# Start-up of a two-layer mixer trunk: the parameter rows copied ahead of the first weight splits, x's squares behind the memory's copies, x spilled in four pieces

## The chip, the cores and the metric

The kernel runs on one core of one Trainium2 chip, as one program. The metric is its time on the device in microseconds (us), from one launch with all inputs in the chip's memory. Beside the times there is one profiled execution, of which every instruction is recorded.

The engines of a core that the text speaks of: TensorE (PE, matmuls and transposes), VectorE (DVE), ScalarE (ACT), GpSimd (POOL) and SyncE (SP, which here only issues transfers). PSUM is the memory that matmuls write to. Each engine takes its own instructions in the order of its queue.

## The reference, cut to what matters

Two layers; x is 512 tokens of 1024 numbers, `mem` is 256 tokens of 1024.

```python
def reference(x, mem, positions, norm_mix, w_in, ..., mem_norm, mem_w_kv, ...):
    mem_n = rmsnorm(mem, mem_norm)
    for l in range(2):
        x = hybrid_layer(x, mem_n, ...)

def hybrid_layer(x, mem_n, ...):
    h = rmsnorm(x, norm_mix)
    (...) = split_cols(h @ w_in)                       # 1024 x 9416
    ...                                                # four branches y_a, y_b, y_c, and:
    mk, mv = jnp.split(mem_n @ mem_w_kv, 2, axis=-1)   # 1024 x 1024
    mk = rmsnorm(mk.reshape(b, 256, 4, 128), mem_k_norm)
    ...                                                # y_m: attention of x's queries to mk, mv
    x = x + merged @ w_out
    hf = rmsnorm(x, norm_ffn)
    gate, up = jnp.split(hf @ ffn_w_up, 2, axis=-1)
    return x + (jax.nn.silu(gate) * up) @ ffn_w_down
```

The change concerns what comes before the first `h @ w_in`: the normed memory, its keys and values for both layers, and the first `h`.

## The kernel before, in words

**Products.** Every fp32 matrix product is done in three matmuls (`mm3`, lines 284 to 286): both operands are split in a high part (rounded to the matmul's format) and a low part (the rest), and hi·hi, hi·lo and lo·hi are summed in PSUM. So each weight and each activation passes through a split: ScalarE writes the high part by a copy, VectorE writes the low part by a subtraction.

**Weights.** `Chunk` loads 1024 x 256 weights (1 MB) by SyncE's queue into `w_raw` (two buffers). It is split in two halves of 4 rows of tiles each, `w_hi` on ScalarE and `w_lo` on VectorE, each with three buffers, so a split waits until TensorE has done with the half three before it. `A()` (line 119) is the helper through which every ScalarE operation goes, so that line stands for them all; the tiles tell them apart.

**Start-up.** The parameter rows (norm gains and the like) come by small loads into `rows`, one transpose (line 184) brings them into PSUM, and a ScalarE copy writes them to `prm`, one column to each 128 channels. Then, as the program is written:

- `mem_in_T()`: the memory is transposed (line 402) in eight steps. Each step writes `mt_hi` (ScalarE, scaled by a column of `prm`) and `mt_lo` (VectorE). The first step's scaling thus needs `prm`.
- `mem_kv(0)` with `first_h()`, step about, then `rope_tables()` and `mem_kv(1)`, all of which share the engines. Each `mem_kv` runs over four weight chunks, eight in all ("chunk 1" to "chunk 8"). A chunk is multiplied with both 128-token halves of the memory (`tokens`), 24 matmuls of 128x256 for each, 48 a chunk, 384 in all. For keys, ScalarE copies the result out of PSUM into `ku`, it is normed, transposed back, and split into `kv`; for values it is split into `kv` straight from PSUM. The results take turns in three PSUM tiles (`mm`). The finished `kv` goes out to memory on ScalarE's queue.
- `first_h()`: x is loaded into `xin` (two loads). ScalarE squares it in four instructions that also sum (written to `mem_sq`, sums to `xs`); from the sums come `rstd`, and four small matmuls spread it (line 429). Then for each of eight chunks x is transposed (line 436), copied to `xc`, and split into `h_hi` and `h_lo` (`h_chunk`, line 297). At the end `xc`, 2 MB, is stored to `x_spill` by one transfer on ScalarE's queue (line 441), to be read back for the residual.

Then the first layer's mixer begins: chunks of `w_in`, multiplied with `h`, with 128x512 matmuls.

**What sets the order.** The program's text names tiles and operations; a list scheduler with a model of the engines' times puts each engine's instructions in a row before the kernel is compiled. `tc.high_priority(offset=AHEAD)` lets the weight splits and the `ku` copies be chosen ahead of what is written before them. The row that comes out is fixed: on the chip an engine waits at an instruction whose input is not there, whatever stands behind it.

Of the kernel before, what the change touches and what calls it, by code (L numbers as in the profile page):

```python
# [16 lines left out]
AF = mybir.ActivationFunctionType  # L17
# [7 lines left out]
D = 1024  # L25
KD = D // P
DEPTH = 2
MEM = 256
# [41 lines left out]
def hybrid_trunk(ctx: ExitStack, tc: tile.TileContext, x, mem, positions, norm_mix, w_in, conv_w,  # L70
                 dsa_q_norm, dsa_k_norm, hgrn_lower_bounds, hgrn_out_norm, mem_norm, mem_w_kv,
                 mem_q_norm, mem_k_norm, w_lift, w_out, norm_ffn, ffn_w_up, ffn_w_down, out):
    nc = tc.nc
# [33 lines left out]
    order = mybir.DependencyInfo(mybir.DependencyClass.NoSync, mybir.DependencyReason.DATA)  # L107
# [4 lines left out]
    def A(dst, src, func, **kw):  # L112
        name = tables.get(func)
        if name is not None and name != table["set"]:
            load = act.preload_act_table_set(name)
            for u in table["users"]:
                tc.add_manual_dep(load.ins, u.name, order, reason="table set")
            table.update(set=name, load=load.ins, users=[])
        i = act.activation(dst, src, func, **kw)  # L119
        if name is not None:  # L120
            tc.add_manual_dep(i.ins, table["load"].name, order, reason="table set")
            table["users"].append(i.ins)
        return i
# [7 lines left out]
    def tr_ps():  # L131
        return bank["tr"]()

    def f(ap):
        return ap.bitcast(F32)
# [28 lines left out]
    ps = tr_ps()  # L164
# [3 lines left out]
    n_rows = 78  # L168
# [13 lines left out]
    prm = consts.tile([P, n_rows], F32, name="prm")  # L182
    ps = tr_ps()
    pe.transpose(ps[:, :n_rows], rows[:n_rows, :], ident[:n_rows, :n_rows])
    A(prm, ps[:, :n_rows], AF.Copy)

    def g_mix(l, c):
        return prm[:, l * KD + c:l * KD + c + 1]
# [4 lines left out]
    def g_mem(c):  # L193
        return prm[:, 32 + c:33 + c]
# [28 lines left out]
    def rstd_into(dst, ms, scratch, n):  # L223
        rstd(dst, ms, scratch(n), scratch(n))

    def small(n, name="small", bufs=12):
        return consts.tile([P, 8], F32, name=name, bufs=bufs)[:, :n]
# [8 lines left out]
    class Chunk:  # L236
        def __init__(self, src, kt, n):
            self.kt, self.step = kt, min(kt, 1024 // n)
            raw = wpool.tile([P, 2048], F32, name="w_raw", bufs=RAW_BUFS)[:, :kt * n].rearrange("p (k n) -> p k n", n=n)
            nc.sync.dma_start(raw, src.rearrange("(k p) n -> p k n", p=P))  # L240
            self.parts = []
            for k in range(0, kt, self.step):
                e = min(kt, k + self.step)
                m = (e - k) * n
                hi, lo = (wpool.tile([P, 1024], F32R, name=nm, bufs=W_BUFS)[:, :m].rearrange("p (k n) -> p k n", n=n)
                          for nm in ("w_hi", "w_lo"))
                with tc.high_priority(offset=AHEAD):
                    A(hi, raw[:, k:e], AF.Copy)
                    dve.tensor_sub(lo, raw[:, k:e], f(hi))  # L249
                self.parts.append((range(k, e), hi, lo))  # L250

        def at(self, k):
            hi, lo = self.parts[k // self.step][1:]
            return hi[:, k % self.step, :], lo[:, k % self.step, :]
# [33 lines left out]
    x_dram = nc.dram_tensor("x_spill", [P, KD, S], F32, kind="Internal").ap()  # L288
# [6 lines left out]
    def h_chunk(h, ssq, c, gain, xs):  # L295
        A(h[0][:, c, :], xs, AF.Copy, scale=gain)
        dve.scalar_tensor_tensor(h[1][:, c, :], xs, gain, f(h[0][:, c, :]), op0=OP.mult, op1=OP.subtract)
        if ssq is not None:
            square(ssq, c, xs)
# [94 lines left out]
    mem_sq = sp.tile([P, D], F32, name="mem_sq")  # L394
    mt = (sp.tile([P, KD, MEM], F32R, name="mt_hi"), sp.tile([P, KD, MEM], F32R, name="mt_lo"))
    mem_r2, mem_r4 = small(4, name="mem_r2", bufs=1), small(4, name="mem_r4", bufs=1)

    def mem_in_T():
        for c in range(KD):
            ps = tr_ps()  # L400
            for t in range(2):
                pe.transpose(ps[:, t * P:(t + 1) * P], mem_in[:, t, c * P:(c + 1) * P], ident)
            A(mt[0][:, c, :], ps[:, :MEM], AF.Copy, scale=g_mem(c))
            dve.scalar_tensor_tensor(mt[1][:, c, :], ps[:, :MEM], g_mem(c), f(mt[0][:, c, :]),
                                     op0=OP.mult, op1=OP.subtract)
        for t in range(2):
            A(mem_sq, mem_in[:, t, :], AF.Square, scale=D ** -0.5, accum_out=mem_ss[:, t:t + 1])
        rstd_into(mem_r, mem_ss, small, 2)
        dve.tensor_copy(mem_r4.rearrange("p (a b) -> p a b", b=2), mem_r[:, :, None].to_broadcast([P, 2, 2]))
        dve.tensor_mul(mem_r2, mem_r4, mem_r4)  # L410
# [3 lines left out]
    def first_h():  # L414
        xin = sp.tile([P, NT, D], F32, name="xin")
        for hf in range(2):
            nc.sync.dma_start(xin[:, 2 * hf:2 * hf + 2, :],
                              x[0, hf * 2 * P:(hf + 1) * 2 * P, :].rearrange("(t p) d -> p t d", p=P))
        xs = small(NT, "xs", 1)
        r_t = small(NT, "rstd_t", 2)  # L420
        r_b = state.tile([P, S], F32, name="rstd", bufs=1)
        for t in range(NT):
            A(mem_sq, xin[:, t, :], AF.Square, scale=D ** -0.5, accum_out=xs[:, t:t + 1])
        rstd_into(r_t, xs, small, NT)
        ps = tr_ps()
        for t in range(NT):
            diag = sp.tile([P, P], F32, name="diag", bufs=2)
            dve.tensor_scalar(diag, ident, r_t[:, t:t + 1], float(P), op0=OP.mult, op1=OP.mult)
            pe.matmul(ps[:, t * P:(t + 1) * P], ones_h, diag, start=True, stop=True)
        A(r_b, ps, AF.Copy)  # L430
        norms.extend((r_t, r_b))
        xc = sp.tile([P, KD, S], F32, name="xc")
        for c in range(KD):
            ps = tr_ps()
            for t in range(NT):
                pe.transpose(ps[:, t * P:(t + 1) * P], xin[:, t, c * P:(c + 1) * P], ident)
            A(xc[:, c, :], ps, AF.Copy)
            h_chunk(h, None, c, g_mix(0, c), xc[:, c, :])
            if c % 2:
                yield  # L440
        nc.scalar.dma_start(x_dram, xc)

    def mem_kv(l):
        kv = sp.tile([P, 4, 2, 2, MEM], F32R, name="kv", bufs=1)
# [29 lines left out]
        for q in range(2):  # L474
# [8 lines left out]
            nc.scalar.dma_start(kv_dram[l][:, 2 * q:2 * q + 2, 1], f(kv[:, 2 * q:2 * q + 2, 1]))  # L483
            yield
    mem_in_T()
    steps(mem_kv(0), first_h())
    rope_tables()
    steps(mem_kv(1))
# [861 lines left out]
```

## Time and profile before

| | |
|---|---|
| time, median of 3 runs | 2039.63 us (2039.58 to 2039.97) |
| the profiled execution's own time | 2039.99 us |
| its span in the profile | 2038.3 us |
| mean clock granted to TensorE | 0.994 of full speed |
| TensorE busy | 2011.1 us (99% of the span), 10440 matmuls |
| VectorE busy | 1418.7 us (70%) |
| ScalarE busy | 1112.4 us (55%) |
| moved by the DMA queues | 226.93 MB, 111 GB/s on average |

The profile of one execution gives the busy time of each engine, the groups of instructions by line and tile, the waits of an engine with what ended them, and the chain of waits: the work that ended last, followed back from the end, at each step to what released it. The timeline lists an engine's instructions with start and duration. Where neighbours of one kind follow closely they stand in one row with a count, and the records of neighbours overlap a little. A table by windows gives for stretches of the span how long each engine was busy, the clock granted to TensorE and what the transfers moved.

### The profile page before, as it was taken

Reading aid. Unit: us, or ns where it says so; the run is one execution under the profiler, and the core shown is the slowest. Engines: PE = TensorE matmul, PEld = TensorE weight load, DVE = VectorE, ACT = ScalarE, POOL = GpSimd, SP = SyncE. Lnnn points to the kernel's source line nnn. Section 1 sums busy time; section 2 is a strip of 40 time slices with the busy share of each in tenths; the row PEclk is TensorE's granted clock in tenths of the full one; section 3 lists DMA queues with packets and bytes.
Section 4 is the critical chain, followed back from the end, with each engine's and each line's share of the span. In section 5 each row is a group of like instructions: output and inputs, shape, how many; then the busy total and the mean of one; then the engine's idle time right before and its main releaser. Section 6 shows DMA issues by size and latency. Waiting matters only on the chain.

```text
span 2038.3 us, 27510 instructions
## 1 busy us (share of the span) xinstructions
PE 2011.1 (99%) x10440; PEld 1695.1 (83%) x10440; DVE 1418.7 (70%) x2721; ACT 1112.4 (55%) x1978; POOL 68.9 (3%) x84
## 2 busy tenths in 40 slices
PE   7899999999999999999999999999999999999999
PEld 7898988888888878888889898878888887888887
DVE  5668899636766778547656889964677577863772
ACT  6554565866666555324445455577667655542541
POOL 1000000000000011001000000000000001000100
PEclk8899999999999999999999999999999999999999
DMA  6632122212224475525352222221222337563442
GB/s 222 231 94 89 57 94 93 94 63 66 90 73 144 113 198 133 146 93 135 98 176 72 91 78 94 94 93 42 83 73 83 129 112 186 151 156 103 104 114 93
DMA packets 177847, 226.93 MB, mean 111 GB/s; under 512 B 5922, under 2 KB 131956, under 8 KB 177588
## 3 DMA queue, kind: packets, MB, share of 16 engines
q1 hardware_dynamic: 160800, 193.55, 29.0%
q0 software_dynamic: 13312, 23.21, 7.0%
q10 hardware_dynamic: 3604, 8.43, 1.1%
q8 instruction: 82, 1.34, 0.3%
q14 instruction: 49, 0.40, 0.1%
HBM read 214.67 MB, written 10.49 MB: 110 GB/s over the span
## 4 chain that ended last, share of the span: by engine, by line
PE 94%; DMA 3%; DVE 1%; ACT 1%; issue 0%; POOL 0%; SPq 0%; ACTq 0%; DVEq 0%; POOLq 0%
PE mm L284 19%; PE mm L285 18%; PE mm L286 18%; PE B L285 4%; PE B L286 4%; PE B L284 4%; PE A L286 4%; PE A L284 4%; PE A L285 4%; PE C L285 2%; PE C L284 2%; PE C L286 2%; DMA w_raw<-in_ffn_w_up_dram 1%; PE tr L734 1%; PE tr L728 1%; PE at L705 1%
## 5 line engine op out<-in xcount | busy, mean ns | idle before, releaser
L119 ACT ACTIVATE w_hi<-w_raw 128x1024 fp32r<-128x1024 f32 (+1 forms) x362 | 373.5, 1033 | 448.3 <-PE mm L285 137.4
L249 DVE TENSOR_TENSOR w_lo<-w_raw,w_hi 128x1024 fp32r<-128x1024 f32 x258 | 311.8, 1209 | 224.4 <-ACT w_hi L119 221.1
L284 PE MATMUL mm<-h_hi,w_hi 128*128 128x512 f32 x960 | 378.7, 395 | 0.0
L285 PE MATMUL mm<-h_lo,w_hi 128*128 128x512 f32 x960 | 377.3, 393 | 0.0
L286 PE MATMUL mm<-h_hi,w_lo 128*128 128x512 f32 x960 | 375.3, 393 | 0.0
L284 PEld LDWEIGHTS mm<-h_hi,w_hi 128*128 128x128 f32 x960 | 180.5, 188 | 37.4 <-issue 2.0
L286 PEld LDWEIGHTS mm<-h_hi,w_lo 128*128 128x128 f32 x960 | 180.4, 188 | 37.3 <-issue 0.7
L285 PEld LDWEIGHTS mm<-h_lo,w_hi 128*128 128x128 f32 x960 | 180.5, 188 | 36.7 <-issue 1.7
L1132 DVE TENSOR_TENSOR w_lo<-w_raw,w_hi 128x1024 fp32r<-128x1024 f32 (+1 forms) x104 | 117.8, 1138 | 61.4 <-ACT w_hi L119 61.2
L286 PE MATMUL mm<-w_hi,h_lo 128*128 128x256 f32 (+1 forms) x448 | 127.9, 286 | 0.0
L284 PE MATMUL mm<-w_hi,h_hi 128*128 128x256 f32 (+1 forms) x448 | 127.1, 285 | 0.0
L285 PE MATMUL mm<-w_lo,h_hi 128*128 128x256 f32 (+1 forms) x448 | 126.9, 284 | 0.0
L284 PE MATMUL mm<-y_hi,w_hi 128*128 128x512 f32 x256 | 102.3, 401 | 0.0
L286 PE MATMUL mm<-y_hi,w_lo 128*128 128x512 f32 x256 | 101.5, 397 | 0.0
L285 PE MATMUL mm<-y_lo,w_hi 128*128 128x512 f32 x256 | 101.3, 396 | 0.0
L119 ACT ACTIVATE w_hi<-f_raw 128x1024 fp32r<-128x1024 f32 (+1 forms) x64 | 62.7, 980 | 60.8 <-PE B L286 38.5
L286 PEld LDWEIGHTS mm<-w_hi,h_lo 128*128 128x128 f32 x448 | 85.6, 191 | 1.4 <-issue 0.8
L284 PEld LDWEIGHTS mm<-w_hi,h_hi 128*128 128x128 f32 x448 | 85.2, 191 | 1.2 <-issue 0.8
L285 PEld LDWEIGHTS mm<-w_lo,h_hi 128*128 128x128 f32 x448 | 85.4, 191 | 0.7
L1132 DVE TENSOR_TENSOR w_lo<-f_raw,w_hi 128x1024 fp32r<-128x1024 f32 (+1 forms) x64 | 71.6, 1120 | 11.8 <-ACT w_hi L119 11.4
L119 ACT ACTIVATE prob<-prob,small 128x128 f32<-128x128 f32 (+3 forms) x128 | 69.2, 554 | 15.4 <-DVE small L717 14.8
L285 PE MATMUL B<-w_lo,s_hi 128*128 128x512 f32 (+1 forms) x192 | 71.7, 375 | 1.1 <-DVE w_lo L1132 1.1
(425 smaller groups left out, 4563.6 us busy)
## 6 DMA issues: line engine op xcount, KB each, us to landing
w_raw<-in_w_in_dram SPq DMA_DIRECT2D x72, 1024.0 KB, 5.1
w_raw<-in_ffn_w_up_dram SPq DMA_DIRECT2D x60, 512.0 KB, 4.5
w_raw<-in_ffn_w_down_dram SPq DMA_DIRECT2D x18, 1024.0 KB, 5.6
w_raw<-in_w_lift_dram SPq DMA_DIRECT2D x32, 512.0 KB, 3.4
w_raw<-in_ffn_w_up_dram POOLq DMA_DIRECT2D x24, 512.0 KB, 6.0
f_raw<-in_ffn_w_up_dram SPq DMA_DIRECT2D x20, 512.0 KB, 4.5
w_raw<-in_mem_w_kv_dram SPq DMA_DIRECT2D x8, 1024.0 KB, 7.8
w_raw<-in_w_out_dram SPq DMA_DIRECT2D x8, 1024.0 KB, 5.1
```

The source lines that it names most:

```text
L119: i = act.activation(dst, src, func, **kw)
L249: dve.tensor_sub(lo, raw[:, k:e], f(hi))
L284: pe.matmul(ps, ah, bh, start=first, stop=False, skip_group_check=go_on)
L285: pe.matmul(ps, ah, bl, start=False, stop=False, skip_group_check=go_on)
L286: pe.matmul(ps, al, bh, start=False, stop=last, skip_group_check=go_on)
L705: pe.matmul(ps, q[:, hh, s], k[1][:, :n], start=False, stop=True)
L728: pe.transpose(pp[:, (2 * e + i) * P:(2 * e + i + 1) * P], probs[2 * i + e][:, b * P:(b + 1) * P], ident)
L734: pe.matmul(pv[e * HD:(e + 1) * HD, :], vt[:, b, :], pt[:, b, e * 2 * P:(e + 1) * 2 * P], start=b == 0, stop=b == t)
L1132: dve.tensor_sub(lo, self.raw[:, 2 * i:2 * i + 2, :], f(hi))
```

## The change

Two things are changed. First, three orders between ScalarE's instructions are laid down for the scheduler, as dependencies that fix an order and add no wait between engines: the `w_hi` splits of chunk 1 come behind the copy to `prm`; every later `w_hi` split, and the four squares of `xin`, come behind the last `mt_hi` copy. Second, `xc` is stored in four transfers of 512 KB, each issued after the two chunks that it holds, where it was one of 2 MB at the end.

```diff
-    A(prm, ps[:, :n_rows], AF.Copy)
+    first = {"prm": A(prm, ps[:, :n_rows], AF.Copy)}
+
+    def behind(i, *names):
+        for n in names:
+            tc.add_manual_dep(i.ins, first[n].ins.name, order, reason="first work")
...
                 with tc.high_priority(offset=AHEAD):
-                    A(hi, raw[:, k:e], AF.Copy)
+                    behind(A(hi, raw[:, k:e], AF.Copy), "mt" if "w" in first else "prm")
                     dve.tensor_sub(lo, raw[:, k:e], f(hi))
                 self.parts.append((range(k, e), hi, lo))
+            first["w"] = True
...
-            A(mt[0][:, c, :], ps[:, :MEM], AF.Copy, scale=g_mem(c))
+            first["mt"] = A(mt[0][:, c, :], ps[:, :MEM], AF.Copy, scale=g_mem(c))
...
         for t in range(NT):
-            A(mem_sq, xin[:, t, :], AF.Square, scale=D ** -0.5, accum_out=xs[:, t:t + 1])
+            behind(A(mem_sq, xin[:, t, :], AF.Square, scale=D ** -0.5, accum_out=xs[:, t:t + 1]), "mt")
...
             h_chunk(h, None, c, g_mix(0, c), xc[:, c, :])
             if c % 2:
+                nc.scalar.dma_start(x_dram[:, c - 1:c + 1, :], xc[:, c - 1:c + 1, :])
                 yield
-        nc.scalar.dma_start(x_dram, xc)
```

The diff moves lines by up to five: L240 becomes L244, L249 L253, L441 L445. The rows that the scheduler makes differ on each engine in the start-up and the first part of the first mixer only.

ScalarE at the start, before, from the first small norm operation of the memory (`small`) on. `w_hi_215` and `w_hi_219` are chunk 1's halves; `mem_sq, xs <- xin` are the squares of x.

```order
L119 ACTIVATE small_203<-mem_ss_154,eps_82 128x2
L119 ACTIVATE w_hi_215<-w_raw_213 128x1024
L119 ACTIVATE w_hi_219<-w_raw_213 128x1024
L119 ACTIVATE small_203<-small_203,half_84 128x2
L119 ACTIVATE small_204<-small_203 128x2
L119 ACTIVATE mem_sq_156,xs_314<-xin_311 128x1024 x3
L119 ACTIVATE prm_132<-tr_133 128x78
L119 ACTIVATE mem_sq_156,xs_314<-xin_311 128x1024
L119 ACTIVATE mt_hi_157<-tr_161,prm_132 128x256
```

The same place now, as far as the first square. Eight `mt_hi` copies stand between chunk 1's splits and chunk 2's; their last three end the first piece shown here.

```order
L119 ACTIVATE small_203<-mem_ss_154,eps_82 128x2
L119 ACTIVATE small_203<-small_203,half_84 128x2
L119 ACTIVATE small_204<-small_203 128x2
L119 ACTIVATE prm_132<-tr_133 128x78
L119 ACTIVATE w_hi_215<-w_raw_213 128x1024
L119 ACTIVATE w_hi_219<-w_raw_213 128x1024
L119 ACTIVATE mt_hi_157<-tr_161,prm_132 128x256
```

```order
L119 ACTIVATE mt_hi_157<-tr_186,prm_132 128x256
L119 ACTIVATE mt_hi_157<-tr_191,prm_132 128x256
L119 ACTIVATE mt_hi_157<-tr_196,prm_132 128x256
L119 ACTIVATE w_hi_362<-w_raw_360 128x1024
L119 ACTIVATE w_hi_366<-w_raw_360 128x1024
L119 ACTIVATE mem_sq_156,xs_314<-xin_311 128x1024
```

The copy to `prm` has moved ahead of chunk 1's splits and of all squares; the squares have moved behind the eight `mt_hi` copies and both halves of chunk 2 (`w_hi_362`, `w_hi_366`). On VectorE, chunk 1's two `w_lo` now stand ahead of the first `mt_lo`:

```order
L253 TENSOR_TENSOR w_lo_216<-w_raw_213,w_hi_215 128x1024
L253 TENSOR_TENSOR w_lo_220<-w_raw_213,w_hi_219 128x1024
L409 SCALAR_TENSOR_TENSOR mt_lo_158<-tr_161,prm_132,mt_hi_157 128x256
```

Before, they stood ahead of it too, with nine rows of other small work between the second and the `mt_lo`; now none.

ScalarE near the end of the start-up, before. `w_hi_978` is chunk 8's second half, `w_hi_1103` the first half of the first `w_in` chunk, `ku_877` the copy that frees the PSUM tile which chunk 8's first 24 matmuls (`mm_982`) need.

```order
L119 ACTIVATE h_hi_152<-xc_342,prm_132 128x512 x2
L441 DMA x_spill<-xc_342 128x4096
L119 ACTIVATE w_hi_978<-w_raw_972 128x1024
L119 ACTIVATE kv_710<-mm_917,mem_r_155 128x2x128
L119 ACTIVATE kv_710<-mm_944,mem_r_155 128x2x128
L119 ACTIVATE w_hi_1103<-w_raw_1101 128x1024
L119 ACTIVATE ku_877<-mm_852 128x256
```

The same place now, where the numbers are three or so higher (`w_hi_981`, `w_hi_1106`, `ku_880`), from the third piece of the spill to the fourth:

```order
L445 DMA x_spill<-xc_342 128x1024
L119 ACTIVATE w_hi_981<-w_raw_975 128x1024
L119 ACTIVATE xc_342<-tr_622 128x512
L119 ACTIVATE xc_342<-tr_630 128x512
L119 ACTIVATE kv_713<-mm_920,mem_r_155 128x2x128
L119 ACTIVATE h_hi_152<-xc_342,prm_132 128x512
L119 ACTIVATE w_hi_1106<-w_raw_1104 128x1024
L119 ACTIVATE kv_713<-mm_947,mem_r_155 128x2x128
L119 ACTIVATE kv_713<-tr_801,prm_132 128x256
L119 ACTIVATE h_hi_152<-xc_342,prm_132 128x512
L119 ACTIVATE ku_880<-mm_855 128x256
L445 DMA x_spill<-xc_342 128x1024
```

The last two `xc` copies and the last `h_hi` copies, all ahead of chunk 8's second half before, now stand behind it; the split of `w_in` still stands ahead of the `ku` copy, with two `kv` copies and one `h_hi` between. The tile that this `ku` copy frees is now needed by chunk 8's second 24 matmuls (`mm_1012`); the first 24 (`mm_985`) wait for VectorE alone. The first piece of the spill stands ahead of chunk 7's second half, the second and third behind chunk 8's first half, the fourth behind the `ku` copy.

## The prediction

> **What bounds the kernel.** I read the page first, then TensorE's waits, then the chain of waits in its first 90 us, because the diff touches only the start-up. "Kept busy" below means that the rows show no gap.
>
> ```profile
> span 2038.3 us, 27510 instructions
> PE 2011.1 (99%) x10440; PEld 1695.1 (83%) x10440; DVE 1418.7 (70%) x2721; ACT 1112.4 (55%) x1978; POOL 68.9 (3%) x84
> PE 94%; DMA 3%; DVE 1%; ACT 1%; issue 0%; POOL 0%; SPq 0%; ACTq 0%; DVEq 0%; POOLq 0%
> PE tr L402 <- ACT prm L119: 6.5, 1, 6.5
> PE mm L284 <- ACT ku L119: 5.9, 1, 5.9
> PE tr L468 <- DVE ku L464: 1.2, 1, 1.2
> 84.00:90.00 6.00, 6.00 (x33) 4.92 (x32) 5.54 (x23) 2.56 (x5) 0.00 (x0) 1.00 0.56 172
> ```
>
> TensorE is busy 99% of the span and carries 94% of the chain. So an edit pays only where TensorE stands still. Its waits (engine and line, who released it, us in total, times, longest) show two long ones in the start-up: 6.5 us for the ScalarE copy that writes `prm`, and 5.9 us for a ScalarE copy that writes `ku`. From 84 us on it is full at clock 1.00 (columns of the last row: PE, weight loads, VectorE, ScalarE, GpSimd, granted clock, DMA share, GB/s). Behind that point the order of the program is soon the old one, so I count no change there: what the first mixer matmul gains, the end gains.
>
> **Step 1, the start: `prm` ahead of the squares.** ScalarE's and TensorE's timelines (start, duration, instruction, idle before):
>
> ```profile
> 10.41 0.36 PE L184 MATMUL tr<-ident,rows 78*128 78x78 f32 x1 [3.45 <-DMA rows<-n_hgrn_lower_bounds_dram]
> 11.22 2.00 ACT L119 ACTIVATE w_hi<-w_raw 128x1024 fp32r<-128x1024 f32 x2 [1.93 <-DMA w_raw<-in_mem_w_kv_dram]
> 16.79 1.06 ACT L119 ACTIVATE mem_sq<-xin 128x1024 f32<-128x1024 f32 x1 [0.36 <-DMA xin<-in_x_dram]
> 17.84 0.22 ACT L119 ACTIVATE prm<-tr 128x78 f32<-128x78 f32 x1
> 19.02 0.82 ACT L119 ACTIVATE mt_hi<-tr,prm 128x256 fp32r<-128x256 f32 x2
> 19.53 0.58 PE L284 MATMUL mm<-w_hi,mt_hi 128*128 128x256 f32 x1 [0.73 <-ACT mt_hi L119]
> ```
>
> The transposed parameter rows are in PSUM at about 10.8 (10.41 + 0.36). The copy to `prm` starts at 17.84, because ScalarE takes its queue in order and three squares of `xin` stand ahead, the third of which waits for its load until 16.79. In the new order stand `prm`, the two `w_hi` of chunk 1, then the `mt_hi` copies. The `w_hi` splits still wait for their load at 11.22 and take 2.00; the first `mt_hi` thus starts near 13.2 instead of 19.02, 5.8 us earlier.
>
> Two pieces come off. On VectorE the first `mt_lo` stands behind chunk 1's two `w_lo`, which run straight ahead of it when `mt_hi` comes this early; I take 0.4 for the matmul that reads it. Chunk 2's first split stood behind three `mt_hi` copies and now stands behind all eight; a split takes about 1.0 us, half of which the 48 matmuls of chunk 1 should hide: 0.5. Together 0.9, bounds 0 and 1.5 (none hidden, and 0.5 for `mt_lo`). The slow clock of the first matmuls is the same on both sides. **Step 1: 5.8 − 0.9 = 4.9 us.**
>
> **Step 2, the squares.** They move into a stretch in which TensorE is full, so they need room on ScalarE (groups with count, busy us, mean ns and idle before; then a window's row, a row of the chain, and two matmuls from the end of this stretch):
>
> ```profile
> L119 ACT ACTIVATE w_hi<-w_raw 128x1024 fp32r<-128x1024 f32 x18 | 19.0, 1059 | 9.7 <-DMA w_raw<-in_w_in_dram 6.1 <-DMA w_raw<-in_mem_w_kv_dram 2.3 <-PE mm L286 1.2
> L119 ACT ACTIVATE mem_sq<-xin 128x1024 f32<-128x1024 f32 x4 | 4.2, 1056 | 0.8 <-DMA xin<-in_x_dram 0.8
> L119 ACT ACTIVATION_READ_ACCUMULATOR mem_sq<-xin 128x1 f32 x4 | 0.7, 187 | 0.0
> 20.00:30.00 10.00, 10.00 (x74) 10.00 (x74) 6.84 (x24) 5.00 (x12) 0.00 (x0) 0.83 0.13 41
> 62.35 1.23 DVE w_lo L249
> 68.02 0.28 PE L285 MATMUL mm<-w_lo,mt_hi 128*128 128x256 f32 x1
> 68.14 0.28 PE L286 MATMUL mm<-w_hi,mt_lo 128*128 128x256 f32 x1
> ```
>
> 4.2 + 0.7 = 4.9 us in records that overlap a little. Where they land ScalarE has been busy 5.00 of 10 us (20 to 30), so the idle half of that stretch hides them. The risk is position: they stand between splits. A chunk's second half is needed 24 matmuls after its first, 24 × 0.12 = 2.9 us (the pitch of the two matmul rows); its `w_hi` and `w_lo` take 1.06 + 1.23 = 2.3. One square of 1.06 + 0.19 ahead of it oversteps that by 0.6, unless the split started early. With four squares the cost lies between 0 and 4.9; I take 0.3, near the lower end, because the stretch has 5 us free. The chain norms → `rstd` → `xc` starts later too, but is not on the path: first matmuls on `h` come only after 384 matmuls.
>
> **Step 3, the second stall: the spill and the first w_in chunk.**
>
> ```profile
> 57.65 0.45 PE tr L436 x4
> 61.10 0.27 ACT ku L119
> 61.37 0.96 ACT w_hi L119
> 63.61 11.37 DMA w_raw<-in_w_in_dram
> 64.13 0.34 ACTq L441 DMA_DIRECT2D x_spill<-xc  x1
> x_spill<-xc ACTq DMA_DIRECT2D x1, 2048.0 KB, 10.7
> w_raw<-in_mem_w_kv_dram SPq DMA_DIRECT2D x8, 1024.0 KB, 7.8
> w_raw<-in_mem_w_kv_dram SPq DMA_DIRECT2D x1, 1024.0 KB, 5.1
> 75.06 1.06 ACT L119 ACTIVATE w_hi<-w_raw 128x1024 fp32r<-128x1024 f32 x1 [6.13 <-DMA w_raw<-in_w_in_dram]
> 76.03 0.37 ACT L119 ACTIVATE ku<-mm 128x256 f32<-128x256 f32 x1
> 76.45 0.58 PE L284 MATMUL mm<-w_hi,mt_hi 128*128 128x256 f32 x1 [5.93 <-ACT ku L119]
> 71.00:72.00 1.00, 0.00 (x0) 0.00 (x0) 0.00 (x0) 0.00 (x0) 0.00 (x0) 0.58 1.14 485
> 81.00:82.00 1.00, 1.00 (x9) 1.00 (x9) 0.63 (x5) 0.21 (x1) 0.00 (x0) 0.80 0.00 0
> 84.47 0.40 PE L284 MATMUL mm<-h_hi,w_hi 128*128 128x512 f32 x1
> ```
>
> The first rows are the chain's (start, us, what), then come an issue and three groups of issues (the last of 28 to 34 us alone), timelines and windows. They read: behind a `w_lo` (the chain's row above) a `w_raw` buffer comes free at 63.6, the w_in load goes out, and 0.5 us later the whole 2 MB spill goes out beside it. The load takes 11.37 us (the eight mem_w_kv loads: median 7.8). Its split stands ahead of a `ku` copy on ScalarE; that copy would free the PSUM tile which chunk 8's first matmul needs. So TensorE ends at 68.3 and resumes at 76.45: 8.2 us, less 0.45 for four `ku` transposes in the gap (the duration of the L436 row): 7.7. Then the clock: it falls to 0.50 at about 71.2 (0.58 over 71 to 72) and is back at about 81.4 (0.80 over 81 to 82). The last 48 matmuls took 84.47 − 76.45 = 8.02 us; at 0.12 each they take 5.76: 2.26 lost. **The stall costs 7.7 + 2.3 = 10.0 us.**
>
> What of it stays? I walk the new order forward with these durations (successive ScalarE records overlap by about 0.1 us, so each is taken 0.1 shorter than its mean):
>
> ```profile
> 66.81 1.07 ACT L119 ACTIVATE w_hi<-w_raw 128x1024 fp32r<-128x1024 f32 x1
> L119 ACT ACTIVATE h_hi<-xc,prm 128x512 fp32r<-128x512 f32 x8 | 5.6, 728 | 0.0
> L119 ACT ACTIVATE xc<-tr 128x512 f32<-128x512 f32 x8 | 4.4, 596 | 0.6 <-PE tr L436 0.6
> L119 ACT ACTIVATE kv<-mm,mem_r 128x256 fp32r<-128x256 f32 x7 | 3.3, 473 | 3.7 <-PE mm L286 3.7
> ```
>
> Chunk 8's second split started at 66.81, when TensorE's 324th matmul freed a `w_hi` buffer; with the 4.9 us won before it, 61.9. Chunk 7's second split is freed 48 matmuls (5.8 us) and some three or four sets of transposes (0.45 each) earlier: 54.6, with its `w_lo` done at 56.9. The w_in load then goes out near 57.0 (63.61 before). One 512 KB piece of the spill is out by then, two more go out while it flies, the last behind the split. With 5.1 us (the load at 29 us, alone on the queues) to 7.8 it lands at 62.1 to 64.8. ScalarE goes on from 61.9 with the split (0.97), two `xc` (0.49 each), a `kv` copy (0.4) and `h_hi` (0.61): at 64.9 it comes to the split of w_in, and behind it (0.97) two `kv` copies (0.36 each), `h_hi` (0.61) and `ku` (0.27) end at 67.5. TensorE ends its 336th matmul 4.9 us before 68.3, at 63.3, now needs that tile only for chunk 8's second 24 matmuls: the first 24 (2.9) and four transposes (0.45) bring it there at 66.6. Left: **about 1.1 us with the hand-over, gain 10.0 − 1.1 = 8.9 us**; so short a gap should leave the clock alone (before, it fell 2.9 us after the last matmul). Bounds: 10.0 with no wait, and rival A's 3.2.
>
> The four issues instead of one cost ScalarE's queue 0.34 us each by the L441 row, three more: 1.0 us beside its work, inside the 64.9 (bounds 0 and 1.0 on the path).
>
> **Sum.** 4.9 − 0.3 + 8.9 = 13.5 us. The profiled execution took 2039.99 us in itself (span 2038.3 and 1.7 around it), 0.4 above the median of the runs, 2039.63. From the median: **2026.1 us** (the profiled one would be 2026.5). Best bounds, all in full: 5.8 + 10.0 = 15.8, and 1.0 for a start that also saves clock time: 2022.8.
>
> [...] TensorE's clock returned about 3.9 us after matmuls began at 19.53 (0.83 over 20 to 30, the row in step 2) and about 5 us after 76.45. [...]
>
> **Rivals.** One window more, the one in which the first spill pieces would fly:
>
> ```profile
> 50.00:60.00 10.00, 10.00 (x88) 10.00 (x87) 6.14 (x10) 7.71 (x22) 0.00 (x0) 1.00 0.75 249
> ```
>
> (A) The w_in load stays as slow as before: 11.4 us from 57.0 is 68.4, the split starts 3.5 later than my 64.9, TensorE waits 4.6 and the clock falls once more (2.2). For it: three spill pieces and a load fly together, as before. Against: pieces of 512 KB, and 2 of them after the load is well on its way. Gain 4.9 − 0.3 + (10.0 − 6.8) = 7.8: 2031.8 us.
> (B) The squares are paid in full: 4.9 − 4.9 + 8.9 = 8.9: 2030.7 us. For it: 10.00 of 10 us of TensorE from 20 on, nothing to spare if the splits are late. Against: ScalarE's free 5.00.
> (C) Only the start gains. For it: the split of w_in still stands ahead of the `ku` copy, so if load and TensorE move forward by the same 4.9 us, the stall stays. Against: the load goes out 6.6 earlier by the walk, and 24 matmuls have come ahead of the tile. 4.9 − 0.3 = 4.6 us: 2035.0.
> (D) Slower: each spill piece flies beside a weight load and delays it; four loads, each late by 11.4 − 5.1 = 6.3 us (the w_in load against the 1 MB load alone), cost 25 us, less 13.5: 2051 us. It decides from about 3.4 us a load beyond what the two raw buffers hide. Against: the stretch 50 to 60 moved 249 GB/s, and the one beside the spill 485 in its best microsecond.
>
> (E) No effect: ScalarE's later queue gives the start back before 84, within 0.2% (4.1 us, about what a measurement of this kernel can tell from no change).
>
> **Chances.** Forecast 0.68 (2022.8 to 2029), A 0.12, B 0.11, C 0.03, E 0.03, D 0.03. C lies just past 0.2%, so faster is 0.68 + 0.12 + 0.11 + 0.03 = 0.94. The range takes in forecast, B and A: 2022.8 to 2032.5.
>
> **What would show it.** Right: `prm` copied near 11, first `mm` L284 near 13.7 (19.53), the w_in load out near 57 and landed within 8 us, TensorE's wait for `ku` about 1 us with no dip of the clock, the first matmul on `h_hi` near 71 (84.47). Wrong: waits of TensorE for `w_hi` or `w_lo` between 20 and 60 (B), a `ku` wait of over 3 us with the clock at 0.50 behind it (A), loads of 9 us and more all along (D), or a new wait after 84.

## The result: 13 us faster, as forecast, and the profile after

The changed kernel takes 2026.83 us (median of four runs, 2026.35 to 2026.96) beside 2039.80 for the kernel before (2039.58 to 2041.19): a ratio of 0.9935, with an interval of 0.9923 to 0.9947. The forecast was 2026.1. The profiled execution took 2026.35 us.

The page's first lines and TensorE's waits up to 100 us (who waited, for whom, us, times, longest):

```profile
span 2024.6 us, 27521 instructions
PE 2006.8 (99%) x10440; PEld 1691.8 (84%) x10440; DVE 1419.2 (70%) x2721; ACT 1113.0 (55%) x1978; POOL 69.0 (3%) x84
PE tr L184 <- DMA rows<-n_hgrn_lower_bounds_dram: 4.9, 1, 4.9
PE mm L289 <- ACT mt_hi L119: 1.6, 1, 1.6
PE mm L289 <- DVE kv L487: 1.4, 1, 1.4
```

Both long waits are gone: the 6.5 us for `prm` and the 5.9 us for `ku`. What is left is the landing of the parameter rows, 1.6 us for the first `mt_hi`, and 1.4 us ahead of chunk 8, for a `kv` on VectorE.

The timelines at the places that the prediction spoke of:

```profile
11.12 0.24 ACT L119 ACTIVATE prm<-tr 128x78 f32<-128x78 f32 x1 [1.20 <-PE tr L184]
11.47 2.01 ACT L119 ACTIVATE w_hi<-w_raw 128x1024 fp32r<-128x1024 f32 x2
13.89 0.58 PE L289 MATMUL mm<-w_hi,mt_hi 128*128 128x256 f32 x1 [1.60 <-ACT mt_hi L119]
56.89 0.37 SPq L244 DMA_DIRECT2D w_raw<-in_w_in_dram  x1
65.39 1.07 ACT L119 ACTIVATE w_hi<-w_raw 128x1024 fp32r<-128x1024 f32 x1
65.91 0.39 PE L289 MATMUL mm<-w_hi,mt_hi 128*128 128x256 f32 x1 [1.37 <-DVE kv L487]
67.66 0.41 ACT L119 ACTIVATE ku<-mm 128x256 f32<-128x256 f32 x1
71.76 0.40 PE L289 MATMUL mm<-h_hi,w_hi 128*128 128x512 f32 x1
86.82 0.36 PE L289 MATMUL at<-mk,qg_hi 128*128 128x256 f32 x1
w_raw<-in_w_in_dram SPq DMA_DIRECT2D x1, 1024.0 KB, 5.1
w_raw<-in_w_in_dram SPq DMA_DIRECT2D x4, 1024.0 KB, 5.5
x_spill<-xc ACTq DMA_DIRECT2D x4, 512.0 KB, 4.3
70.00:80.00 10.00, 10.00 (x54) 8.57 (x53) 8.98 (x46) 4.13 (x7) 0.00 (x0) 1.00 0.81 278
```

`prm` is copied at 11.12 (17.84 before) and the first product starts at 13.89 (19.53). The first w_in load goes out at 56.89 (63.61) and lands in 5.1 us (11.4), the four of the start in a median of 5.5, each piece of the spill in 4.3. The first matmul on `h` is at 71.76 (84.47): 12.7 us of the gain stand there already. The last row has TensorE full at clock 1.00 where it had stood and then run at 0.50.

Two later points proved useful. The first matmul on `mk`, the memory's keys read back from memory for the first layer, is at 86.82 now and 100.23 before, 13.4 us earlier; 0.7 us of that is order, since six matmuls fewer stand ahead of it (456; 462). The first matmul on `qS`, the queries of a later branch, has the same 1874 matmuls and transposes ahead of it in every kernel of this document, and from 110 us to there TensorE is full in all of them; it tells what the start is worth. Before and now:

```profile
323.82 0.22 PE L704 MATMUL at<-k_hi,qS 128*128 128x128 f32 x1
311.09 0.22 PE L709 MATMUL at<-k_hi,qS 128*128 128x128 f32 x1
```

It is 12.7 us earlier, as the first matmul on `h` is.

### The profile page after: what moved, and what is told of

It is laid out like the page before. It is cut to its first block, busy times and chain, and to the rows that moved or that the text cites. A ratio compares the mean times of both kernels' runs of the same rounds, so it can differ in the third digit from the quotient of the medians.

```text
span 2024.6 us, 27521 instructions
## 1 busy us (share of the span) xinstructions
PE 2006.8 (99%) x10440; PEld 1691.8 (84%) x10440; DVE 1419.2 (70%) x2721; ACT 1113.0 (55%) x1978; POOL 69.0 (3%) x84
## 4 chain that ended last, share of the span: by engine, by line
PE 95%; DMA 2%; DVE 1%; ACT 1%; issue 0%; POOL 0%; SPq 0%; ACTq 0%; POOLq 0%; DVEq 0%
PE mm L289 18%; PE mm L290 18%; PE mm L291 18%; PE B L290 5%; PE B L291 5%; PE B L289 5%; PE A L289 4%; PE A L291 4%; PE A L290 4%; PE C L290 2%; PE C L289 2%; PE C L291 2%; DMA w_raw<-in_ffn_w_up_dram 1%; PE tr L739 1%; PE tr L733 1%; PE at L710 1%
## 5 line engine op out<-in xcount | busy, mean ns | idle before, releaser
L253 DVE TENSOR_TENSOR w_lo<-w_raw,w_hi 128x1024 fp32r<-128x1024 f32 x258 | 311.9, 1210 | 210.5 <-ACT w_hi L119 207.0
```

## The experiments

The runs were made on several chips, and on the later ones the same kernel varied by 1 to 9 us between executions (the kernel before: 2040 to 2048). So ratios are to the kernel before on the same chip, and causes are read from the profiles up to the first matmul on `qS`. In this table, in us from the span's start: the first product, the first matmul on `h`, the issue of the first `mk` load, TensorE's wait for it, the first matmul on `mk` (456 to 469 matmuls stand ahead of it, most of them 0.12 us each), the first on `qS`. The first product alone varies by 0.8 us (18.89 to 19.71) between kernels with the same order up to there.

| kernel | first product | on `h` | `mk` issued | wait for `mk` | on `mk` | on `qS` | ratio (interval) |
|---|---|---|---|---|---|---|---|
| before | 19.53 | 84.47 | 93.36 | 0 | 100.23 | 323.82 | 1 |
| changed | 13.89 | 71.76 | 80.15 | 0 | 86.82 | 311.09 | 0.9935 (0.9923 to 0.9947) |
| three orders, one spill | 13.56 | 71.05 | 82.99 | 2.0 | 89.56 | 316.11 | 0.9946 (0.9931 to 0.9961) |
| four pieces alone | 19.71 | 77.01 | 86.83 | 0.6 | 92.86 | 317.15 | 0.9962 (0.9948 to 0.9977) |
| squares behind `prm` alone | 15.98 | 75.72 | 84.10 | 0 | 90.77 | 315.08 | 0.9939 (0.9924 to 0.9954) |
| squares twice | 13.08 | 69.93 | 78.85 | 0 | 85.16 | 309.46 | 0.9932 (0.9916 to 0.9949) |
| `ku` first | 18.94 | 76.72 | 90.25 | 2.6 | 96.80 | 323.58 | 1.0004 (0.9993 to 1.0015) |
| spill late | 18.94 | 75.76 | 87.26 | 0 | 93.30 | 315.14 | 0.9965 (0.9953 to 0.9978) |
| four pieces at the end | 18.89 | 76.59 | 88.29 | 3.7 | 96.11 | 322.97 | 0.9985 (0.9976 to 0.9994) |
| changed, two more orders | 13.03 | 71.64 | 80.02 | 0 | 86.69 | 310.93 | 0.9937 (0.9924 to 0.9949) |
| ... and loads held | 11.43 | 70.33 | 79.13 | 1.3 | 86.78 | 311.07 | 0.9917 (0.9903 to 0.9930) |
| ... and `mk` early | 11.63 | 70.71 | 72.38 | 0 | 85.77 | 310.04 | 0.9925 (0.9912 to 0.9939) |

### The three orders without the pieces

```diff
-                nc.scalar.dma_start(x_dram[:, c - 1:c + 1, :], xc[:, c - 1:c + 1, :])
                 yield
+        nc.scalar.dma_start(x_dram, xc)
```

> The changed kernel with the spill in one piece of 2 MB again; the three orders on ScalarE stay. ScalarE's row is otherwise that of the changed kernel, the one spill stands behind the ku copy. Theory (the second stall went because the w_in load goes out 6 to 7 us earlier and ScalarE's row was shuffled): the load flies alone from about 57, TensorE's wait before chunk 8 stays near 1.4, time 2026.8 (2026 to 2028), as changed. Rival (the pieces are what took the second stall away): the w_in load or the next one is slowed as before, 4 to 6 us come back, 2031 to 2033.

The wait ahead of chunk 8 did not come back, and the first matmul on `h` is as early as in the changed kernel. But part of the gain is lost behind it, at the load that the rival had named as the next one, and by way of a wait that neither had named. The chain of waits, from 60 us (start, us, what), and the rows behind it:

```profile
64.56 13.50 DMA w_raw<-in_w_in_dram
78.09 1.07 ACT w_hi L119
82.99 6.52 DMA mk<-kv
64.90 0.34 ACTq L446 DMA_DIRECT2D x_spill<-xc  x1
89.56 0.58 PE L289 MATMUL at<-mk,qg_hi 128*128 128x256 f32 x1 [2.04 <-DMA mk<-kv]
88.00:89.00 1.00, 0.00 (x0) 0.00 (x0) 0.42 (x1) 0.00 (x0) 0.00 (x0) 0.50 0.94 338
```

The 2 MB go out at 64.90, 0.3 us behind the second w_in load, which then takes 13.50 us. Its split, the third and fourth w_in loads and the `mk` loads behind them on SyncE's queue are late in turn; TensorE waits 1.0 us for a ScalarE square and 2.0 us for `mk`, and its clock is at 0.50 from 88 to past 94. The slow load has moved one load further, and its price with it. At `qS` this kernel is 5.0 us behind the changed one (316.11; 311.09), within the rival's 4 to 6 us: that is what the pieces are worth, given the orders. The times alone don't show it, since the two ratios lie 2 us apart and their intervals overlap.

### The four pieces without the orders

```diff
             if c % 2:
+                nc.scalar.dma_start(x_dram[:, c - 1:c + 1, :], xc[:, c - 1:c + 1, :])
                 yield
-        nc.scalar.dma_start(x_dram, xc)
```

> The kernel before with the spill in four pieces, none of the three orders. prm is copied near 17.8 and the first matmul is at 19.5 as before, so the start gains nothing. Theory (each half of the change is by itself enough to remove the second stall, through the load's speed here): the w_in load has one piece beside it, not 2 MB, lands within 7 us, and the ku copy is no longer what chunk 8's first 24 matmuls wait for; 8 to 9 us gained, 2031 (2029.5 to 2032.5). Rival (the load's earlier issue is what counts): load and stall as before, 2039 to 2040.

```profile
PE mm L284 <- DVE kv L482: 1.4, 1, 1.4
PE at L284 <- DMA mk<-kv: 0.6, 1, 0.6
64.53 7.26 DMA w_raw<-in_w_in_dram
```

The load is issued no earlier than before (64.53; 63.61) and lands in 7.26 us; the second stall has shrunk to 1.4 us, the same that the changed kernel has. The first matmul on `h` is 7.5 us earlier, on `qS` 6.7, the time 0.38%, 7.8 us. So the theory holds: the pieces alone take most of the stall away, without the earlier issue that the forecast relied on. Two things changed at once here, the load's speed and ScalarE's row, in which chunk 8's first 24 matmuls no longer need the `ku` copy behind the split; the run with the spill late, below, has the faster load alone.

### The squares behind `prm`, and nothing else

```diff
-            A(mem_sq, xin[:, t, :], AF.Square, scale=D ** -0.5, accum_out=xs[:, t:t + 1])
+            behind(A(mem_sq, xin[:, t, :], AF.Square, scale=D ** -0.5, accum_out=xs[:, t:t + 1]), "prm")
```

> The kernel before with one order alone: the squares of xin behind the copy to prm (not behind the mt_hi copies), the w_hi splits free, the spill in one piece. prm now stands behind chunk 1's two w_hi and ahead of all squares, but three squares stand between the mt_hi copies. Theory: prm copied near 13.5, first matmul near 15.5 to 16, start gain 3 to 4; the spill still flies beside the w_in load, TensorE waits 3 to 4 us for ku and the clock dips: second stall 4 to 6 instead of 10; in all 2032 (2029.5 to 2035). Rival (the start's gain is lost again at the second stall, which ends with the load): 2038 to 2040.

The first product was at 15.98, as expected, 3.6 us earlier. The second stall disappeared altogether, which was not expected: 8.8 us at the first matmul on `h`, with the spill in one piece. The spill went out at 62.19 here, 2.3 us ahead of the w_in load (before: 0.5 us behind it), and the load took 7.9. That its lead is the reason fits with the other runs, but was not tried by itself, and there is a rival: the rows below, ScalarE's, put the split of w_in (72.99) behind a `kv` copy that waits for TensorE, so that the load had landed (72.4) before ScalarE came to it, and chunk 8's first 24 matmuls were done.

```profile
72.62 0.48 ACT L119 ACTIVATE kv<-mm,mem_r 128x256 fp32r<-128x256 f32 x1 [2.77 <-PE mm L290]
72.99 1.05 ACT L119 ACTIVATE w_hi<-w_raw 128x1024 fp32r<-128x1024 f32 x1
```

At `qS` this one order, with the spill in one piece, brings 8.7 of the 12.7 us, net of some 1.5 us lost to the slow clock, which came once more from 22.5 to 25.9; the 1.5 is an estimate from the kernel before, where the 128x256 matmuls stood 0.21 us apart at clock 0.50 and 0.12 at 1.00 (77 to 84 us). Its ratio (0.9939) can't be told from the changed kernel's (0.9935).

### Every square twice

```diff
         for t in range(NT):
-            behind(A(mem_sq, xin[:, t, :], ...), "mt")
+            for _ in range(2):
+                behind(A(mem_sq, xin[:, t, :], ...), "mt")
```

> The changed kernel with every square of xin made twice (four more squares of 1.06 + 0.19 us on ScalarE, 4.7 to 4.9 us in all; the second one writes the same numbers). Theory (squares are hidden in ScalarE's free time once TensorE is fed): 2026.8 to 2028.5. Rival (squares behind TensorE's weights cost in full, and the four of the change already do): 2031 to 2032.

ScalarE's groups from 10 to 84 us, of the changed kernel and of this one (busy us, mean ns, idle before):

```profile
L119 ACT ACTIVATE mem_sq<-xin 128x1024 f32<-128x1024 f32 x4 | 4.2, 1055 | 0.0
```

```profile
L119 ACT ACTIVATE mem_sq<-xin 128x1024 f32<-128x1024 f32 x8 | 8.4, 1053 | 0.0
```

4.2 us more on ScalarE, and from the first product to the first matmul on `h` 56.85 us instead of 57.87. The squares are hidden; the ratio, 0.9932, is that of the changed kernel (0.9935) within the intervals. Rival B falls.

### `ku` ahead of the late split

```diff
+            seen["chunks"] += 1
...
-                    A(hi, raw[:, k:e], AF.Copy)
+                    i = A(hi, raw[:, k:e], AF.Copy)
+                    if seen["chunks"] == 9:
+                        tc.add_manual_dep(i.ins, seen["ku"].ins.name, order, reason="ku first")
...
-                    A(ku.rearrange("p a b -> p (a b)"), ps, AF.Copy)
+                    seen["ku"] = A(ku.rearrange("p a b -> p (a b)"), ps, AF.Copy)
```

> The kernel before with one order: both splits of the first w_in chunk behind the last ku copy. The ku copy thus changes places with the split that waits for the load; spill, loads and start stay. Theory (TensorE stood because ku was queued behind a split whose load was late): TensorE goes on at 68.8 without the 5.9 us wait and at full clock, ends chunk 8 near 74.6, and then waits for the w_in load itself (landed at 75.0, split at 76.1): first matmul on h near 76.5 instead of 84.47, 8 us gained. Rival (the load is the whole of the stall, whatever stands where): the wait moves to the first matmul on h and with it the clock, under 3 us gained.

```profile
PE tr L472 <- DVE ku L468: 1.2, 1, 1.2
PE at L288 <- DMA mk<-kv: 2.6, 1, 2.6
63.98 11.22 DMA w_raw<-in_w_in_dram
76.72 0.40 PE L288 MATMUL mm<-h_hi,w_hi 128*128 128x512 f32 x1
94.00:95.00 1.00, 0.17 (x2) 0.00 (x0) 0.33 (x2) 0.75 (x5) 0.00 (x0) 1.00 1.10 405
96.00:97.00 1.00, 0.20 (x1) 0.20 (x2) 0.00 (x0) 0.00 (x0) 0.00 (x0) 0.79 0.45 166
97.00:98.00 1.00, 1.00 (x6) 1.00 (x6) 0.00 (x0) 0.00 (x0) 0.00 (x0) 0.50 0.08 29
103.00:104.00 1.00, 1.00 (x9) 1.00 (x9) 0.23 (x1) 0.00 (x0) 0.00 (x0) 0.80 0.00 0
```

This is the run that tells most. At the first matmul on `h` the theory is right to 0.2 us: 76.72, 7.75 us earlier than before. And the time is the same as before, 1.0004, as is the first matmul on `qS` (323.58; 323.82). The load still takes 11.22 us, the w_in loads and `mk` behind it are issued nearly as late as before (`mk` at 90.25; 93.36), TensorE waits 2.6 us for `mk`, and then runs at half its clock from 96.6 to about 103.4. What is gained ahead of `mk` without moving the loads is given back at `mk`.

### The spill late, and the spill in four at the end

Both are the kernel before with the spill moved. In the first it is one transfer behind the last `ku` copy; in the second it is in four pieces, all behind the last `xc` copy.

```diff
-        nc.scalar.dma_start(x_dram, xc)
+        seen["xc"] = xc
...
+    spill = nc.scalar.dma_start(x_dram, seen["xc"])
+    tc.add_manual_dep(spill.ins, seen["ku"].ins.name, order, reason="late spill")
```

```diff
-            A(xc[:, c, :], ps, AF.Copy)
+            done = A(xc[:, c, :], ps, AF.Copy)
...
-        nc.scalar.dma_start(x_dram, xc)
+        for c in range(0, KD, 2):
+            piece = nc.scalar.dma_start(x_dram[:, c:c + 2, :], xc[:, c:c + 2, :])
+            tc.add_manual_dep(piece.ins, done.ins.name, order, reason="at the end")
```

> The kernel before with the one spill of 2 MB issued behind the last ku copy, so that the first w_in load flies without it. Theory (the load took 11.4 us because of the spill): it lands in 5.5 to 7 us, near 69.5 to 70.5, ku ends near 71.5, TensorE waits 2 to 3 us instead of 7.1 and its clock stays up: first matmul on h near 77.5; but the spill then flies beside the second and third w_in loads as in the run with one spill, and 3 to 6 us come back before 100 us: in all 2 to 5 us gained. Rival (the load is slow for another reason): 11 us again, no gain.

> The kernel before with the spill in four pieces of 512 KB, all of them behind the last xc copy (at 60 to 66 us), not as the chunks are made; the ku copy comes ahead of the w_in split here, as in the run with ku first, which is the one to compare with. Theory (2 MB of spill beside the first w_in loads is what counts, in one piece or four): loads of 10 us or so, first matmul on h near 76.7, then TensorE waits 2 to 3 us for mk and its clock dips, first matmul on mk near 96 to 97, no gain or 1 us. Rival (a small transfer gets out of the way of a load, a large one does not): w_in loads of 6 to 7 us, no wait for mk, first matmul on mk near 92 to 93, 7 us gained.

With the spill late, issued at 69.49, the first w_in load has landed by 68.3 and the stall is gone; the second w_in load takes 10.6 us, but TensorE does not wait for it or for `mk`. 8.7 us are gained at `qS` and 0.35%, 7 us, in time: more than the 2 to 5 expected, because with the late start this slow load is still hidden. The split of w_in and the `ku` copy behind it stand in ScalarE's row as before. So it was the spill that made the first w_in load slow and, through it, the second stall.

With four pieces at the end the first w_in load takes this long (the issue of that microsecond alone), and TensorE waits for `mk`:

```profile
w_raw<-in_w_in_dram SPq DMA_DIRECT2D x1, 1024.0 KB, 9.8
PE at L284 <- DMA mk<-kv: 3.7, 1, 3.7
```

9.8 us, as against 11.22 with one piece at the same place and 7.26 with the pieces spread out. So the theory holds in the main: here the size of a piece counted less than how much of the spill was on the queues when the load was issued. At `qS` 0.9 us are gained, as expected (0 to 1); the time is 0.15% less than before, 3 us (0.06 to 0.24%).

### What the start still waits for, and a try at a better version

Three runs build on the changed kernel. The first puts `xin`'s loads behind chunk 2's load and chunk 1's second split half behind the second `mt_hi`; the second also holds both loads until `mem_in` has landed; the third also puts the `mk` loads ahead of the fourth w_in load.

```diff
+                for i in first.pop("xin"):
+                    tc.add_manual_dep(i.ins, load.ins.name, order, reason="xin late")
...
-                    behind(A(hi, raw[:, k:e], AF.Copy), "mt" if "w" in first else "prm")
+                    behind(A(hi, raw[:, k:e], AF.Copy), "mt" if "w" in first else "mt1" if k else "prm")
...
+                pool.tensor_copy(raw[:, 0, 0:1], mem_in[:, 1, D - 1:D])
...
+            pool.tensor_copy(xin[:, 2 * hf, 0:1], mem_in[:, 1, D - 1:D])
...
+                tc.add_manual_dep(load.ins, first["mk"].ins.name, order, reason="mk early")
```

> The changed kernel with two more orders: xin's two loads behind chunk 2's load on SyncE's queue, and the second half of chunk 1's split behind the second mt_hi copy. Nothing else moves on ScalarE. Theory (the start now waits for chunk 1's load, which shares the queues with xin, and for two splits in a row ahead of mt_hi): chunk 1 lands 2 to 3 us earlier unless the parameter rows are the last to come; the first matmul is near 11.5 to 12.5 instead of 13.9 and TensorE waits 1.4 to 2.4 us less: 2024.5 (2023.5 to 2026). Rival (the squares and xc then come too late for the mixer, or the rows land as late as before): 2026.5 to 2028.

> The run with both orders (xin's loads behind chunk 2's, chunk 1's second split half behind the second mt_hi), and in addition chunk 2's load and xin's two loads are held on SyncE's queue until mem_in has landed, by three copies of one column from mem_in on GpSimd into the tiles that the loads then overwrite. Only mem_in, chunk 1 and the small loads are then on the queues for the first 6 us. Theory (the parameter rows come late, at 10.4 to 10.8, because 3 MB more are on the queues with them): rows near 7 to 8.5, prm near 9, first matmul near 10 to 10.5, 3 us earlier than in the changed kernel; ScalarE's row is another from there on and may cost some of it: first matmul on mk at 83 to 86 (86.8 in the changed kernel), 1 to 3 us gained on it. Rival (the rows are late by the latency of small transfers alone): first matmul near 13 as before, no gain.

> The run with the held loads, and on SyncE's queue the two mk loads ahead of the fourth w_in load (they stood behind it and were issued at 79.1, and TensorE waited 1.3 us for them). ScalarE's row and the number of matmuls ahead of the first one on mk stay. Theory (SyncE's queue, w_in loads and then mk, is what TensorE meets next, so that a gain ahead of it is lost there): mk issued near 70 to 73, no wait for it, first matmul on mk near 85.3 to 85.7 instead of 86.8, 0.990 to 0.9915 of the kernel before. Rival (the mk loads wait for a buffer of the start-up, or the fourth w_in load now comes too late): a wait for mk or for w_hi of 1 us or more ahead of 100 us, no gain on the run with held loads.

The first gained nothing to speak of: the rows landed as late as before, the first product was at 13.03 (13.63 in the changed kernel on the same chip). Here the rival was right. In the second the rows come earlier; their transpose, the first product and the wait for `mk`:

```profile
8.85 0.26 PE L184 MATMUL tr<-ident,rows 78*128 78x78 f32 x1 [1.75 <-DMA rows<-n_hgrn_lower_bounds_dram]
11.43 0.80 PE L294 MATMUL mm<-w_hi,mt_hi 128*128 128x256 f32 x2 [1.16 <-ACT mt_hi L119]
PE at L294 <- DMA mk<-kv: 1.3, 1, 1.3
```

With `xin`'s 2 MB issued from 7.60 on (2.31 and 5.24 in the changed kernel) and chunk 2's load at 7.18 (6.62), the rows are there at 8.85 instead of 10.61, and the first product is 2 us earlier than in the changed kernel on the same chip (11.43; 13.45), where 3 was expected. That the loads beside them are why the rows are late isn't shown by this: with nothing held back they were transposed at 9.05 in two runs (three orders with one spill, four pieces alone) and at 10.14 to 11.03 in the ten others. Nor do early rows suffice: with one spill the first product was at 13.56 all the same, because ScalarE stood for chunk 1's load until 11.14 (first row below). With the loads held that load, too, was there earlier (second row).

```profile
11.14 2.00 ACT L119 ACTIVATE w_hi<-w_raw 128x1024 fp32r<-128x1024 f32 x2 [1.36 <-DMA w_raw<-in_mem_w_kv_dram]
9.95 1.06 ACT L119 ACTIVATE w_hi<-w_raw 128x1024 fp32r<-128x1024 f32 x1 [0.25 <-DMA w_raw<-in_mem_w_kv_dram]
```

But the first matmul on `mk` is not earlier (86.78; 86.57): the gain is lost to 1.3 us of waiting for `mk` and to smaller waits. The third removes that wait and reaches `mk` at 85.77, one microsecond earlier, though on another chip; its ratio, 0.9925, misses the 0.990 to 0.9915 expected. In time, the second took 2027.05 us (2024.46 to 2027.56), the changed kernel beside it 2029.70 (2027.57 to 2033.79); the ratios 0.9917, 0.9925 and, for the changed kernel, 0.9934 (0.9921 to 0.9946) overlap. That any of them is faster than the changed kernel isn't shown.

The changed kernel itself was run twice more as a yardstick.

> The changed kernel as it is, once more, beside the runs of this call. 2026.8 where the kernel before takes 2039.6, 0.9935 of it on any chip, and within 0.1% of itself.

> The changed kernel once more beside the runs of this call: first matmul near 13.7, first matmul on h near 72, on mk near 87, 0.9935 to 0.9945 of the kernel before.

Its ratio held both times, 0.9943 (0.9931 to 0.9955) and 0.9934. The 0.1% between its own executions did not: they spread over 5 and 6 us. The profiles put part of it late in the program, at a wait of TensorE for `merged`, a sum that VectorE makes in the feed-forward part. Of the three profiled executions of the changed kernel, the first and the second:

```profile
PE C L289 <- DVE merged L1275: 1.0, 2, 0.7
```

```profile
PE C L289 <- DVE merged L1275: 4.9, 3, 3.2
```

## Why the prediction was right, and where it was right by luck

**Step 1** held. It put the first product near 13.7 and the gain at 5.8 less 0.9; measured were 13.89 and 5.6. TensorE then waits 0.3 us for the first `mt_lo`, at 15.1, and 0.3 us for a `w_lo`, between 20 and 24: the two deductions, a little smaller than booked (0.6; 0.9). That the slow clock cost the same on both sides was luck, as shown below.

**Step 2** held, and its 0.3 us were too much: with twice the squares nothing is lost.

**Step 3** had the right size and half the wrong reason. Its walk was good to half a microsecond at each station: w_in load out at 57.0 (56.89), landed within 5.1 to 7.8 us (5.1), split at 64.9 (65.39), `ku` ended at 67.5 (68.07), a wait of 1.1 us (1.4). Chunk 8's second split came at 62.52, not 61.9: it starts when ScalarE is free, as it did before (the row of 66.81 has no wait ahead of it), and not when a buffer is. And TensorE's remaining wait was ahead of chunk 8's first 24 matmuls, for a `kv` on VectorE, not for `ku` ahead of the second 24: VectorE's queue was not walked. From first product to first matmul on `h` 7.1 us were saved (64.94; 57.87), where 8.9 less steps 1's and 2's deductions makes 7.7.

What failed is a premise ahead of the steps: that behind the first mixer matmul nothing changes, so that what it gains, the end gains. The run with `ku` first gains 7.75 us there and nothing in time. What has to move with it is SyncE's queue, four w_in loads and then `mk`. In every row of the table but the last, the first matmul on `mk` stands 6.0 to 7.8 us behind the issue of the first `mk` load, about the time that this load takes (5.4 us in the kernel before, 6.5 in the changed one, 7.8 with the four pieces at the end). In the rows with no wait for `mk` this load did not bind: TensorE was busy throughout from the first matmul on `h` to there, for 15.06 us in the changed kernel, as in the last row, where `mk` was issued 8 us earlier. But hardly anything was to spare. The change moved that issue by 13.2 us (93.36; 80.15), without which the gain could not have been kept; the prediction never looked at it.

**Which half did what.** At `qS`, the orders alone give 7.7 us, the pieces alone 6.7, both 12.7. The start is the orders' (5.6 at the first product), the second stall is in the main the pieces'; with the three orders and no pieces 5.0 us of it come back, as a slow second load and a wait for `mk`. The pieces are not the only way to be rid of it: the spill late, and the squares behind `prm` alone, did without. Rival A, a w_in load as slow as before, was thus a real danger, at the second load.

**The clock at the start.** In the changed kernel the clock came back at about 17.9, as this row of 17 to 18 us shows, 4.0 us behind the first product and in spite of the wait for `mt_lo` at 15.1. In the second of its profiled executions it came back at 19.2, 5.6 us behind a first product at 13.63 (third row). The last row is the kernel before's, where it came back at 23.36:

```profile
17.00:18.00 1.00, 1.00 (x7) 1.00 (x7) 0.86 (x8) 0.19 (x1) 0.00 (x0) 0.57 1.11 349
15.37 0.69 PE L407 MATMUL tr<-ident,mem_in 128*128 128x128 f32 x2 [0.26 <-DVE mt_lo L409]
19.00:20.00 1.00, 1.00 (x11) 1.00 (x9) 0.23 (x1) 0.47 (x1) 0.00 (x0) 0.89 1.10 348
23.00:24.00 1.00, 1.00 (x9) 1.00 (x9) 0.96 (x8) 0.57 (x2) 0.00 (x0) 0.82 0.00 0
```

So the wait for `mt_lo` cost no clock time that these rows show: 4.0 us to full clock, beside 3.8 in the kernel before. Within each of these profiles the changes of the clock lie whole multiples of 3.41 us apart: in the changed kernel down at 11.03 and up at 17.86 (2 times), in the kernel before up at 23.36, down at 71.16, up at 81.40 (14 and 3 times), with `ku` first up at 24.90, down at 96.58, up at 103.40 (21 and 2 times). In these profiles the clock thus changed only at points of a beat of 3.41 us, and where the first product fell between two points was chance: from it to full clock it took 3.8 us in the kernel before, 4.0 and 5.6 in two executions of the changed kernel, 6.0 with one spill. By the 0.21 and 0.12 us between matmuls at clock 0.50 and 1.00, 1.6 us more at 0.50 are some 0.7 us lost, so single profiles differ by that much without a cause in the kernel. The 2.9 us from the last matmul to the fall, from which step 3 took it that a short gap does no harm, are such a chance too (2.4 and 4.0 in two other runs, below). In the changed kernel the stretch of the beat that ended at 17.86 had the gap of 0.3 us in it (TensorE busy 3.15 of 3.41 us), and the clock came up at its end.

## What to carry to other kernels

Where an engine stands behind a late load, look which transfers are on the queues when that load is issued; a store that nobody waits for can be spread over the time in which its data are made, or issued behind the load: here the two, each alone, were worth about the same (0.9962 and 0.9965). Before a gain is booked for the end, follow the loading queue to the next thing that stands behind it: taking one wait away gained nothing where the queue that feeds the next stage did not move too (`ku` first, 1.0004). And a stall on a copy can be a load's: putting the copy ahead of the waiting split removed the wait, and not a microsecond of time.

## What the runs showed of the hardware

How long a 1 MB load took went in these runs with how much of the store was issued close to it, more than with the size of each transfer: it took 5.1 us with nothing of the store beside it (the kernel before, the load at 29 us), 5.1 with two 512 KB pieces issued 2.3 and 3.3 us behind it (the changed kernel's first w_in load), 7.3 with the spill spread out, 9.8 with four 512 KB pieces issued within 2 us of it, 10.6 to 13.5 with one of 2 MB issued less than 1 us behind it, but 7.9 with one issued 2.3 us ahead.

The landing of small loads varied: the parameter rows, 1 to 12 KB each, were transposed at 9.05 to 11.03 us in twelve profiles with all these loads on the queues, and at 8.85 and 8.81 in two with `xin`'s loads held back.

TensorE's clock changed only at points of the beat of 3.41 us in these profiles, and the time from the last matmul to a fall varied: 2.4 us with `ku` first (94.2 to 96.6), 4.0 with the four pieces at the end. The falls went rather with how much work stood between two points of the beat. These rows are such stretches, with `ku` first, with one spill and in the changed kernel around its wait of 1.4 us:

```profile
93.17:96.58 3.41, 1.00 (x9) 0.80 (x7) 0.49 (x3) 1.30 (x6) 0.00 (x0) 1.00 0.97 356
84.43:87.84 3.41, 2.11 (x17) 1.82 (x16) 3.27 (x14) 3.25 (x6) 0.00 (x0) 1.00 1.05 292
62.24:65.65 3.41, 2.30 (x19) 1.88 (x17) 3.41 (x14) 3.41 (x7) 0.00 (x0) 1.00 0.48 197
```

Behind the first two (1.00 and 2.11 us busy) the clock fell, behind the third (2.30) it stayed. In the second execution of the changed kernel it stayed behind one of 2.04 (63.59 to 67.00), so busy time alone does not tell the two apart, and no limit is shown. With `ku` first it took until 103.4 to come back, though work had begun again at 96.8: by the same two pitches the gap of 2.6 us cost some 3 us more in the clock, an estimate.
